# A hop later, and other queues: moving the substitution, the up weights and the gated stores of a hybrid RWKV-7 trunk

## The chip, the cores and the metric

The kernel runs on one core of a Trainium2 chip. The metric is device time in microseconds, the median of several executions. The core's engines run side by side, each with its own queue in order: TensorE (PE, with its weight loads PEld), VectorE (DVE), ScalarE (ACT), GpSimd (POOL) and SyncE (SP). A DMA is issued by one of the queues, here by SP or by ACT; an issue that waits holds up what is queued behind it on that engine.

## The reference, cut to what matters

One layer, 512 tokens, model width 2048, everything in float32:

```python
h = rms_norm(x, norm_g)
z = h @ w_in                         # r, k, v, two loras of 64 | gate | pool input | pool gate
zs = zs + (token_shift(zs) - zs) * mu
w_loglog = -softplus(-(w0 + tanh(wd) @ w_up)) - 0.5
decay = exp(-exp(w_loglog))
a = sigmoid(a0 + ad @ a_up)          # w_up, a_up: the "up weights", 64 x 1024 each
y = wkv7_scan(r, decay, k, v, kk, a) # 16 heads of 64; a delta-rule state, one step a token
y_rwkv = (head_group_norm(y) + bonus) * silu(g_rwkv)
y_pool = (causal_multiscale_pool(u) @ w_pool) * pool_scale * silu(g_pool)
x = x + concat(y_rwkv, y_pool) @ w_out
x = x + sigmoid(x @ w_pg + b_pg) * (p @ w_ple)
return rms_norm(x, final_g)
```

## The kernel before

**Products.** Each large product is made of three float32r matmuls (`mm3`): weights and data are split into a high part and a rest. For a weight chunk (`wsplit`, L127) SP loads `raw`, ACT casts it to `whi` (L132), DVE subtracts to get `wlo` (L133); each has four buffers. The input projection goes by 128 columns at a time (`zcols`), as a generator from which `pump(n)` takes n matmuls to fill the time of PE between the small steps of the recurrence.

**Rounds.** The 16 heads are worked in 8 pairs j. The 512 tokens of a pair are cut into 8 chunks of 64. `recur(j)` (L767) walks the chunks: per chunk a product `py` with the state, whose result DVE makes into `zs` (L799); a product `pu`, copied by ACT to `uv` (L813); a product `ps`, from which DVE makes the next state `sbd` (L825). After each of these three comes a hop: `step()` (L775), then a `pump`. The first chunk has no `py`, so there are 23 hops in a round: the 6th is that after `py` of the third chunk, the 21st that after `py` of the last.

**The substitution.** For the next pair, `scores(j+1)` (L620), run in the second hop, makes the masked products `mt`, writes their diagonal blocks to DRAM (`nd`, L651), and reads them back, copied to all partitions, as two tiles `n` (L656). `invert(j+1)` (L667) inverts 32 triangular blocks of 32x32 by 31 steps of two DVE instructions (L674, L678). `step()` takes them from that generator: from the hop after `HS` on, `HN` at each hop. What a hop takes is put on DVE behind `lead[0]`, the last `zs` or `sbd` (`tc.issue_after` puts what it encloses behind that instruction, on the same engine's queue). When the 31 steps are through, the next call writes the result to DRAM (`xd`, L682) and reads it back as `x1` (L689). `gather(j+1)` (L695) transposes a part of it to `y1` (L732) for the products `pq`, `pmv` and `px`.

**The up weights.** `load_ab(j)` (L348) loads 128 columns of `w_up` and `a_up`, each twice, for the two halves of the partitions, into `ur` and `ar`: four DMAs of 32 KB, issued by ACT. It is called for pair j+1 at the start of `prepare(j)` (L577), which runs ahead of the round of pair j-1. `decay_and_rate(j)` (L519), called from `gather(j-1)`, casts them on ACT (L524, L525) and subtracts on DVE (L526). All these tiles have one buffer.

**Stores.** The gated output of a pair (`gate_out` in `finish`, L893) and of a pool unit (`pool_unit`, L438) go to the DRAM tensor `yd`, 256 KB each, by ACT's queue. `load_y` (L947) reads them, by ACT's queue, for the output projection.

**Order.** PE's order in the rounds is that of the program (`pin`). On the other engines a scheduler orders the instructions when the program is built; it takes what is ready by its own estimate of times, and the program's order and `tc.high_priority` decide between ready ones. On the chip each queue then keeps that order, whatever comes late.

## Time and profile before

| | |
|---|---|
| median of 3 runs | 1085.23 us |
| the runs | 1085.23, 1083.53, 1088.02 us |
| the profiled execution | 1082.7 us |
| its span, first to last instruction | 1081.0 us |
| granted TensorE clock over the span | 0.998 |
| SP's DMA queue | 112.28 MB, 35.9% of 16 engines' span |
| ACT's DMA queue | 33.56 MB, 9.4% |
| the eight rounds | about 75 to 690 us |
| output projection and per-layer embedding | about 715 to 1081 us |

The times of instructions below come from the profiled execution. A row of a timeline has start and length in us, the engine, the line of the kernel, the operation, output and inputs by the program's names, shapes and count; in square brackets stands how long the engine was idle before it, and for what it waited. SPq and ACTq are DMA issues of these queues. A helper's line stands for all its callers: L157 is every matmul of `mm`.

### The profile page before, as it was taken

How to read it: one execution, taken by the hardware profiler on the slowest of the kernel's cores; microseconds unless marked ns; L12 is line 12 of the kernel's file. 1: busy time of each engine (PE TensorE's matmuls, PEld its weight loads, DVE VectorE, ACT ScalarE, POOL GpSimd, SP SyncE). 2: the span in 40 equal slices, each digit the busy share in tenths (PEclk: the TensorE clock that was granted, in tenths of full speed). 3: DMA queues.
4: the chain of work that ended last, by engine and by line, in shares of the span. 5: the costliest groups of instructions: out<-in, count | busy, mean ns of one | idle time of the engine just before them, and what ended most of it. 6: DMA issues, size and time to landing. Idle time of an engine off the chain costs nothing.

```text
span 1081.0 us, 17106 instructions
## 1 busy us (share of the span) xinstructions
PE 1056.6 (98%) x5996; PEld 872.1 (81%) x5996; DVE 714.0 (66%) x1851; ACT 441.5 (41%) x901; POOL 75.0 (7%) x180
## 2 busy tenths in 40 slices
PE   5999999999999999999999999999999999999996
PEld 4888878888888887878788788888888888888885
DVE  6676978888779789787887857563432424445356
ACT  7633435335335354353352344553222222333337
POOL 2100010110110100200101201000000000000000
PEclk9999999999999999999999999999999999999999
DMA  7434443342634533434435343774434428355434
GB/s 236 117 115 111 139 116 88 116 120 74 168 88 114 144 89 105 120 89 112 106 91 158 100 129 111 239 243 141 171 121 143 166 98 271 122 182 161 169 98 156
DMA packets 212916, 146.94 MB, mean 136 GB/s; under 512 B 68085, under 2 KB 173150, under 8 KB 212830
## 3 DMA queue, kind: packets, MB, share of 16 engines
q1 hardware_dynamic: 192126, 112.28, 35.9%
q10 hardware_dynamic: 20704, 33.56, 9.4%
q8 instruction: 47, 0.77, 0.3%
q14 instruction: 39, 0.32, 0.1%
HBM read 122.21 MB, written 23.07 MB: 134 GB/s over the span
## 4 chain that ended last, share of the span: by engine, by line
PE 91%; DVE 4%; DMA 3%; ACT 2%; issue 1%; ACTq 0%; SPq 0%; DVEq 0%
PE acc_o L157 16%; PE acc_g L157 16%; PE zb L157 14%; PE zv L157 8%; PE zg L157 8%; PE zr L157 8%; PE zk L157 7%; PE py L157 2%; PE pu L157 2%; PE pple L157 2%; PE pm L157 1%; DMA n<-nd 1%; PE pp L157 1%; PE ps L157 1%; DMA xt<-in_x_dram 1%; PE pmv L157 1%
## 5 line engine op out<-in xcount | busy, mean ns | idle before, releaser
L133 DVE TENSOR_TENSOR wlo_g<-raw_g,whi_g 128x512 fp32r<-128x512 f32 x84 | 57.0, 685 | 74.4 <-ACT whi_g L132 72.3
L157 PE MATMUL zb<-hhi,whi_b 128*128 128x512 f32 x256 | 106.0, 414 | 0.0
L133 DVE TENSOR_TENSOR wlo_o<-raw_o,whi_o 128x512 fp32r<-128x512 f32 x64 | 43.9, 690 | 90.9 <-ACT whi_o L132 90.8
L157 PE MATMUL zb<-hhi,wlo_b 128*128 128x512 f32 x256 | 100.4, 392 | 0.0
L157 PE MATMUL acc_o<-whi_o,ylo 128*128 128x512 f32 x256 | 100.2, 391 | 0.0
L157 PE MATMUL acc_o<-whi_o,yhi 128*128 128x512 f32 x256 | 99.9, 390 | 0.0
L157 PE MATMUL zb<-hlo,whi_b 128*128 128x512 f32 x256 | 99.8, 390 | 0.0
L157 PE MATMUL acc_o<-wlo_o,yhi 128*128 128x512 f32 x256 | 99.7, 389 | 0.0
L132 ACT CAST whi_g<-raw_g 128x512 fp32r<-128x512 f32 x84 | 52.0, 621 | 105.3 <-PE acc_g L157 58.9
L157 PE MATMUL acc_g<-whi_g,x2hi 128*128 128x512 f32 x208 | 81.2, 391 | 0.0
L832 POOL TENSOR_SCALAR s0p<-sbd,pw 64x64 f32<-64x64 f32 x96 | 58.0, 604 | 332.0 <-DVE sbd L825 243.5
L157 PE MATMUL acc_g<-wlo_g,x2hi 128*128 128x512 f32 x208 | 80.9, 389 | 0.0
L157 PE MATMUL acc_g<-whi_g,x2lo 128*128 128x512 f32 x208 | 80.6, 389 | 0.0
L132 ACT CAST whi_o<-raw_o 128x512 fp32r<-128x512 f32 x64 | 39.9, 623 | 96.3 <-PE acc_o L157 96.3
L132 ACT CAST whi_b<-raw_b 128x512 fp32r<-128x512 f32 x64 | 39.7, 621 | 86.7 <-PE zb L157 29.2
L133 DVE TENSOR_TENSOR wlo_b<-raw_b,whi_b 128x512 fp32r<-128x512 f32 x64 | 43.6, 683 | 27.3 <-ACT whi_b L132 27.1
L157 PEld LDWEIGHTS zb<-hhi,wlo_b 128*128 128x128 f32 x256 | 48.0, 188 | 10.9
L678 DVE TENSOR_TENSOR xw<-xw,tm 128x60 f32<-128x60 f32 (+24 forms) x248 | 52.1, 210 | 7.0
L157 PEld LDWEIGHTS acc_o<-wlo_o,yhi 128*128 128x128 f32 x256 | 48.1, 188 | 9.9
L157 PEld LDWEIGHTS acc_o<-whi_o,ylo 128*128 128x128 f32 x256 | 48.1, 188 | 9.8
L157 PEld LDWEIGHTS acc_o<-whi_o,yhi 128*128 128x128 f32 x256 | 48.1, 188 | 9.7
L157 PEld LDWEIGHTS zb<-hhi,whi_b 128*128 128x128 f32 x256 | 48.2, 188 | 8.3
(283 smaller groups left out, 2529.6 us busy)
## 6 DMA issues: line engine op xcount, KB each, us to landing
raw_b<-in_w_in_dram SPq DMA_DIRECT2D x64, 256.0 KB
raw_o<-in_w_out_dram SPq DMA_DIRECT2D x64, 256.0 KB
raw_g<-in_w_pg_dram SPq DMA_DIRECT2D x64, 256.0 KB
raw_k<-in_w_in_dram SPq DMA_DIRECT2D x32, 256.0 KB
raw_r<-in_w_in_dram SPq DMA_DIRECT2D x32, 256.0 KB
raw_v<-in_w_in_dram SPq DMA_DIRECT2D x32, 256.0 KB
raw_g<-in_w_in_dram SPq DMA_DIRECT2D x32, 256.0 KB
bkd<-bk SPq DMA_DIRECT2D x8, 512.0 KB
```

The source lines that it names most:

```text
L132: nc.scalar.copy(hi, raw)
L133: nc.vector.tensor_tensor(lo, raw, hi.bitcast(F32), ALU.subtract)
L157: i = nc.tensor.matmul(*a, **k)
L678: nc.vector.tensor_tensor(xw[:, 0:n_, s + 1:32], xw[:, 0:n_, s + 1:32], tm[:, 0:n_, 0:w_], ALU.add)
L832: nc.gpsimd.tensor_scalar(s0p[hc, :], nxt[hc, hc], pcn[hc], None, ALU.mult)
```

## The change

The substitution begins one hop later (`HS` 5 to 6), and at the 21st hop, the 15th of those in which it runs, three steps are taken in place of two. The up weights of the next pair are loaded after `scores` has issued the loads of `n`, behind the second of them on SP, and by SP in place of ACT. The stores of the gated outputs and of the pool branch are issued by SP in place of ACT.

```diff
@@ load_ab
-                nc.scalar.dma_start(out=raw[64 * h:64 * h + 64, :], in_=src[0, :, jc])
+                nc.sync.dma_start(out=raw[64 * h:64 * h + 64, :], in_=src[0, :, jc])
@@ pool_unit
-        nc.scalar.dma_start(out=yd[NJ + m], in_=sgp)
+        nc.sync.dma_start(out=yd[NJ + m], in_=sgp)
@@ prepare
-        if j + 1 < NJ:
-            load_ab(j + 1)
@@ scores
             nb.append(t_)
+        if j + 1 < NJ:
+            with tc.issue_after(n_.ins):
+                load_ab(j + 1)
         bg = rw.tile([P, NCH, 4, 32], F32, name=f"bg{j}", tag="bk")
@@ step
-                    for _ in range(HN):
+                    for _ in range(HN + (hop[0] == HE1)):
                         next(work, None)
@@ gate_out
-                nc.scalar.dma_start(out=yd[j], in_=yo)
+                nc.sync.dma_start(out=yd[j], in_=yo)
@@
-    HS, HN = 5, 2
+    HS, HN, HE1 = 6, 2, 21
```

## The prediction

> **What bounds the kernel now.** I read the page's engine shares first, then the waits of the tensor engine alone, then stretches of the span cut at the rounds over the eight head pairs.

> ```profile
> PE 1056.6 (98%) x5996; PEld 872.1 (81%) x5996; DVE 714.0 (66%) x1851; ACT 441.5 (41%) x901; POOL 75.0 (7%) x180
> ```

> PE has work in 98% of the span, and the order of its matmuls in the rounds is pinned by hand. The span can shorten only where PE stands still, or where its next matmul starts late.

> ```profile
> PE py L157 <- DVE sbd L825: 1.4, 2, 0.9
> PE px L157 <- issue: 1.1, 1, 1.1
> PE pu L157 <- DVE zs L799: 1.0, 2, 0.6
> ```

> ```profile
> 424.00:497.00 73.00, 70.95 (x459) 57.69 (x455) 59.59 (x181) 30.11 (x66) 8.76 (x15) 1.00 0.41 107
> 497.00:573.40 76.40, 75.53 (x489) 62.10 (x489) 62.31 (x181) 31.60 (x67) 7.43 (x15) 1.00 0.45 120
> 573.40:664.00 90.60, 89.88 (x561) 73.60 (x562) 64.45 (x203) 32.39 (x73) 11.80 (x18) 1.00 0.41 113
> ```

> The first view lists engine, waited-for, total us, times, longest: inside the rounds the large waits of PE are for sbd and zs, both made by the vector engine (DVE), and one of 1.1 us that the profile puts down to nothing. The second gives length, then the busy time of PE, its weight loads, DVE, ACT and POOL, the granted clock, the DMA share and GB/s. The three rounds idle 2.05, 0.87 and 0.72 us, 3.64 us together, at a granted clock of 1.00. So everything that this change can take away is a few microseconds of 1082.7; 5.4 us would be 0.5%, about the smallest difference that a measurement of this kernel can tell from none.

> What makes sbd late is seen in the order of DVE in one round:

> ```profile
> 509.02 0.29 DVE L799 TENSOR_TENSOR zs<-py,mv 64x128 f32<-64x128 f32 x1 [1.55 <-PE py L157]
> 509.35 0.69 DVE L133 TENSOR_TENSOR wlo_r<-raw_r,whi_r 128x512 fp32r<-128x512 f32 x1
> 512.26 0.19 DVE L674 TENSOR_TENSOR tm<-i,n 128x31 f32<-128x31 f32 x1 [2.21 <-DMA n<-nd]
> ...
> 513.81 0.19 DVE L674 TENSOR_TENSOR tm<-xw,n 128x29 f32<-128x29 f32 x1
> ...
> 514.48 0.19 DVE L678 TENSOR_TENSOR xw<-xw,tm 128x28 f32<-128x28 f32 x1
> 514.59 0.69 DVE L133 TENSOR_TENSOR wlo_v<-raw_v,whi_v 128x512 fp32r<-128x512 f32 x1
> 515.20 0.59 DVE L825 SCALAR_TENSOR_TENSOR sbd<-ps,pw,s0p 64x64 f32<-64x64 f32 x2
> ```

> After zs of the third chunk (the sixth hop), the first step of the substitution stands at the head of DVE's queue and waits 2.21 us for the load of n. Then come four steps (two of the sixth hop, two of the seventh: both are queued behind the same zs) and only then sbd, for which PE waits:

> ```profile
> 434.37 0.39 PE L157 MATMUL zk<-hhi,wlo_k 128*128 128x512 f32 x1
> 434.60 0.38 PE L157 MATMUL py<-sbd,ar 128*128 128x128 f32 x2
> ...
> 440.58 0.39 PE L157 MATMUL zr<-hhi,wlo_r 128*128 128x512 f32 x1
> 441.02 0.49 PE L157 MATMUL py<-sbd,ar 128*128 128x128 f32 x2
> ...
> 514.59 0.39 PE L157 MATMUL zr<-hhi,wlo_r 128*128 128x512 f32 x1
> 515.85 0.49 PE L157 MATMUL py<-sbd,ar 128*128 128x128 f32 x2 [0.87 <-DVE sbd L825]
> ...
> 589.43 0.39 PE L157 MATMUL zb<-hhi,wlo_b 128*128 128x512 f32 x1
> 590.34 0.49 PE L157 MATMUL py<-sbd,ar 128*128 128x128 f32 x2 [0.52 <-DVE sbd L825]
> ```

> An undisturbed py starts 0.23 us after the matmul before it (434.37 to 434.60). The other three start 0.44, 1.26 and 0.91 us after it: late by 0.21, 1.03 and 0.68 us, 1.92 us in all.

> **The change, part by part.** *The substitution a hop later.* With the start at hop 7, two steps stay behind zs, and the next two go behind sbd of hop 8. The two steps that leave the gap are the stretch from 513.81 to 514.67 (514.48 + 0.19) in the round shown: 0.86 us. The wait for n stays: hop 7 is queued behind the same zs. So sbd comes 0.86 us earlier, and the three late py are worth 0.21 + 0.86 + 0.68 = 1.75 us. Below: nothing, if DVE's queue fills the gap with other work; above: 1.92.

> *Three steps at hop 21.* Of the 31 steps, 30 ran by hop 20 before and one followed at hop 21; now 28 run by then and three follow. That is two steps, 0.86 us at the same price, more before the inverse can leave. It comes back through DRAM to the transposes y1, which PE needs for pq:

> ```profile
> 408.30 0.43 DVE L732 STREAM_TRANSPOSE y<-x 32x256 f32<-32x256 f32 x1
> ```

> ```profile
> 410.64 0.69 PE L157 MATMUL pq<-y,mt 32*32 32x32 f32 x32
> ```

> y1 is ready at 408.73, 1.91 us ahead of pq. A delay of 0.86 us is covered by this; in a round with no cover it costs 0.86 us, 6.0 us over seven. I take 0, since the cover shown is twice the delay.

> *Stores and up weights leave ACT's queue.* They issue there like this:

> ```profile
> 425.97 1.78 ACTq L354 DMA_DIRECT2D ar<-in_a_up_dram  x2
> ```

> ```profile
> 498.09 0.33 ACTq L893 DMA_DIRECT2D yd<-yo  x1
> ```

> A round's four weight DMAs and one store are at most 3.9 us of ACT's queue (4 x 0.89 + 0.33). In the waits of PE above no line names ACT, so by itself this gains 0; at most the 1.1 us of px, if that is ACT's. On SP it adds as much, and a store that waits for yo holds up the loads behind it. Those loads have room:

> ```profile
> 498.69 0.37 SPq L129 DMA_DIRECT2D raw_v<-in_w_in_dram  x1
> ...
> 505.74 1.19 SPq L656 DMA_DIRECT2D n<-nd  x2
> ```

> ```profile
> 510.63 0.42 ACT L813 COPY uv<-pu 64x64 f32<-64x64 f32 x2 [0.68 <-PE pu L157]
> 511.79 0.62 ACT L132 CAST whi_v<-raw_v 128x512 fp32r<-128x512 f32 x1 [0.74 <-PE zr L157]
> ```

> raw_v issues at 498.69 and its cast runs at 511.79, 13.1 us later, and that cast waits for PE, not for its load. The loads of bg, which now stand behind the weights, are read only by the transposes in the last chunk. So SP's extra issue is hidden, 0; without that cover it is up to 3.9 us in each of seven rounds, 27 us. The nd stores and the load of n stay ahead of the weights. The store of yo may come ahead of them, but nd waits for mt, which DVE makes after yo. The stores feed loads in the output projection only.

> *The up weights' casts and subtractions move too.* Their tiles have one buffer. Before, the loads refill them as soon as they are read, so the casts (L524, L525) and subtractions (L526) ran in the crowded stretch before the scores:

> ```profile
> 425.67 0.27 DVE L526 TENSOR_TENSOR as<-ar,as 64x128 fp32r<-64x128 f32 x1
> ```

> Now the loads wait for n's issue and the casts fall into the hops. Two subtractions, 0.54 us, leave the stretch in which DVE made PE wait for zs (1.0 us over two places above). I take 0.5 us from one of them; bounds 0 and 1.0. In the hops they can land ahead of sbd, and take back up to 0.54 us in each late round.

> **Sum:** 1.75 + 0.5 = 2.2 us off 1082.7 (span 1081.0, 1.7 around it): 1080.5. The median of the runs is 1085.2, 2.5 above the profiled execution, with runs from 1083.5 to 1088.0; from the median the forecast is **1083.0 us**.

> [...] The rows first:

> ```profile
> 434.00:435.00 1.00, 1.00 (x7) 0.87 (x6) 0.00 (x0) 0.00 (x0) 0.45 (x1) 1.00 0.26 67
> ```

> While n is in flight and little else, a quarter of the sixteen DMA engines is busy, at 67 GB/s. The two loads of n are 512 KB; at that rate they take 7.8 us, so from an issue at 505.74 the second is in at about 513.5. [...]

> **The rivals.**
> 1. *ACT stands still for the up weights* (the slower side). The weights issue behind n; a cast of them that was placed in ACT's queue for an earlier landing blocks what follows. Place: a cast of L524 ahead of the copy uv (L813), which releases ps:

> ```profile
> 512.52 0.38 PE L157 MATMUL ps<-uv,bkn 128*128 128x128 f32 x2
> ```

> The copy shown ends at 511.05, 1.47 us ahead of ps. Held until 513.5 it ends at 513.92, 2.87 us later, so PE waits 1.40 us in that round. The point: two rounds of seven eat the gain of 2.2. With all seven the time is 1085.2 + 9.8 - 2.2 = 1092.8, and each further microsecond of landing adds 7. For it: DVE's wait of 2.21 us for n shows that a queue here can be ordered for an earlier landing than the chip gives. Against: ACT is busy 41% of the span, and a cast that falls behind the copy waits at no cost until the next one.
> 2. *Nothing moves*: DVE fills the gap before sbd with the moved subtractions and further weight splits, or the last steps make y1 late by what the first ones gain. 1085.2.
> 3. *The shifted queues also dissolve what I leave standing*: all of the 3.64 us of idle time above, the 1.1 of px included. A stop costs more than its idle mark: the two marked py are late by 1.03 and 0.68 with marks of 0.87 and 0.52, 0.16 more each. For the five waits in the view of PE that is 0.8, and the unmarked py adds 0.21: together 4.65, or 1080.6. For it: DVE's crowded stretch is relieved at both ends. Against: the change touches nothing that px waits for except ACT's queue.
> 4. *The change does not do what it says*: with hop 7 behind the same zs the wait for n of 2.2 us remains; then only the two steps count. This is inside the forecast.

> **Chances.** Forecast 0.48, nothing 0.20 (rival 2), more 0.16 (rival 3), slower 0.16 (rival 1); rival 4 has its chance inside the forecast. The range leaves out the larger part of rival 1 and the end of rival 3, and allows for the scatter of the runs: **1078.5 to 1088.5**; the likeliest case alone is 1081.5 to 1084.5. Faster by over 0.5% (below 1079.8): the better part of rival 3 with the scatter of the runs, and a little of the forecast's low end, 0.13. Slower by over 0.5% (above 1090.7): rival 1 in six rounds or more, or in fewer with a later landing, 0.12. Within 0.5%: 0.75.

> **What would show it.** Right: in the seven rounds one pair of steps fewer between zs of the third chunk and sbd, py 0.23 us after its predecessor, the wait for n still there, the idle time of PE in the three stretches near 1.8 (3.64 less the two marks of 1.39 and the 0.5) instead of 3.64, and SP's weight and store issues without a later cast. Wrong: PE waiting for uv's ps or for pu, with ACT or DVE idle for a load of up weights; pq waiting for y1; a raw weight's cast that waits for its load.

## The result, and the profile after

| | before | after |
|---|---|---|
| median of 6 runs each, side by side | 1085.61 us | 1116.88 us |
| the runs | 1083.21 to 1088.02 | 1114.17 to 1118.08 |
| ratio, 95% interval | | 1.0287 [1.0266, 1.0308] |
| span of the profiled execution | 1081.0 us | 1115.8 us |

The change costs 31 us. The forecast was 1083.0 with a range to 1088.5: wrong, in sign and in size. The first line of the page of the changed kernel, and the waits of PE (engine, what it waited for, total us, times, longest):

```profile
PE 1066.7 (96%) x5996; PEld 878.4 (79%) x5996; DVE 714.4 (64%) x1851; ACT 440.3 (39%) x901; POOL 74.4 (7%) x180
```

```profile
PE ps L157 <- ACT uv L814: 25.2, 6, 4.9
...
PE py L157 <- DVE sbd L826: 0.8, 2, 0.6
PE px L157 <- issue: 0.8, 1, 0.8
...
PE pu L157 <- DVE zs L800: 0.7, 2, 0.5
```

The number of instructions is the same on every engine. The waits that the prediction worked with (py, px, pu) have all shrunk. One wait is new, and it alone is 25.2 us: PE waits for `ps`, that is for ACT's copy `uv`, in six rounds. ACT is no busier than before (440.3 us against 441.5), so the copy was late for another reason. The same view of all engines names it:

```profile
ACT uaz L525 <- DMA ur<-in_w_up_dram: 50.4, 7, 9.0
```

Six of these seven waits fall into the rounds; the seventh ends at 92.21, before the first copy `uv`, and costs PE nothing.

One of the six rounds, first on the queues of SP and ACT, then on PE (start, length, engine, line, operation; in brackets the idle time before it and what ended it):

```profile
533.76 1.18 SPq L654 DMA_DIRECT2D n<-nd  x2
534.99 0.52 SPq L354 DMA_DIRECT2D ur<-in_w_up_dram  x1
535.55 0.58 SPq L129 DMA_DIRECT2D raw_v<-in_w_in_dram  x1
536.17 0.52 SPq L354 DMA_DIRECT2D ur<-in_w_up_dram  x1
536.73 1.24 SPq L354 DMA_DIRECT2D ar<-in_a_up_dram  x2
```

```profile
537.52 0.69 ACT L369 ACTIVATE sk<-zk,dprm 128x512 f32<-128x512 f32 x1
543.99 0.30 ACT L525 CAST uaz<-ur 64x128 fp32r<-64x128 f32 x1 [5.77 <-DMA ur<-in_w_up_dram]
544.92 0.30 ACT L524 CAST us<-ur 128x128 fp32r<-128x128 f32 x1 [0.64 <-DMA ur<-in_w_up_dram]
545.25 0.42 ACT L814 COPY uv<-pu 64x64 f32<-64x64 f32 x2
```

```profile
540.55 0.40 PE L157 MATMUL zr<-hhi,wlo_r 128*128 128x512 f32 x1
545.72 0.80 PE L157 MATMUL ps<-uv,bkn 128*128 128x128 f32 x2 [4.78 <-ACT uv L814]
...
549.30 0.63 PE L157 MATMUL zr<-hlo,whi_r 128*128 128x512 f32 x1
549.73 0.60 PE L157 MATMUL zr<-hhi,wlo_r 128*128 128x512 f32 x1
550.16 0.39 PE L157 MATMUL py<-sbd,ar 128*128 128x128 f32 x2
```

The casts of `ur` stand in ACT's queue ahead of `uv`. The second half of `ur` is issued by 536.69 and the cast that needs it can start only at 544.92, 8.2 us later. Until then `uv`, which waits for nothing but its place in the queue, is held, and PE with it. `ps` was due at 540.78 (540.55 and the 0.23 us between matmuls) and starts at 545.72: 4.94 us late.

The stop costs more than its length. After it, matmuls start 0.43 us apart (549.30, 549.73, 550.16) in place of 0.23. From the start of `ps` to that of the next `py` there are 4.44 us and nine matmuls of zr; the same ten steps before the change, from the `ps` at 512.52 to 0.23 us behind the zr at 514.59, took 2.30. So 2.14 us more are lost to the clock. The stretches of the span show it (length; PE, weight loads, DVE, ACT, POOL; granted clock, DMA share, GB/s):

```profile
547.00:550.20 3.20, 3.20 (x9) 2.43 (x9) 1.93 (x7) 0.23 (x2) 0.91 (x2) 0.51 0.34 92
550.20:552.00 1.80, 1.80 (x12) 1.55 (x11) 1.34 (x5) 0.39 (x1) 0.00 (x0) 1.00 0.35 55
```

Granted clock 0.51, then 1.00. The six stops have idle marks of 4.63, 4.72, 4.91, 3.33, 2.86 and 4.78 us; all but the one of 2.86 are followed by such slow matmuls. **The account:** marks 25.2, and 0.16 us each beside the mark, make 26.2. The first thirty matmuls behind each stop take 2.31, 1.67, 1.66, 1.51, 0.76 and 2.14 us longer than the same ones in the run with the casts behind the fourth chunk's copy (below), in which PE runs the same matmuls in the same order without these stops. The 0.76, behind the stop of 2.86, is not the clock but a `py` that waits for `sbd`. These six are 10.1 us, with the stops 36.3 of the 37.0 us between the spans of the two executions (1115.8 and 1078.9). Beside the kernel before, the difference is 34.8 us between the profiled spans and 31 between the medians.

The length of a stop doesn't decide by itself whether slow matmuls follow it: behind one of 2.04 us in another run they did, behind one of 3.08 they didn't (at the end of this text).

The seventh round, which has no cast of up weights (the last load is issued in the sixth), runs as before:

```profile
601.00:692.00 91.00, 90.56 (x565) 74.12 (x564) 67.94 (x208) 33.04 (x74) 12.61 (x18) 1.00 0.44 123
```

PE idles 0.44 us of 91.00 in it, at clock 1.00.

### The profile page after: what moved, and what is told of

It is laid out like the page before. It is cut to its first block, busy times and chain, and to the rows that moved or that the text cites. A ratio compares the mean times of both kernels' runs of the same rounds, so it can differ in the third digit from the quotient of the medians.

```text
span 1115.8 us, 17123 instructions
## 1 busy us (share of the span) xinstructions
PE 1066.7 (96%) x5996; PEld 878.4 (79%) x5996; DVE 714.4 (64%) x1851; ACT 440.3 (39%) x901; POOL 74.4 (7%) x180
## 4 chain that ended last, share of the span: by engine, by line
PE 82%; DMA 8%; DVE 5%; ACT 2%; issue 1%; SPq 1%; ACTq 0%; DVEq 0%
PE acc_g L157 15%; PE acc_o L157 15%; PE zb L157 12%; PE zv L157 8%; PE zr L157 8%; PE zk L157 6%; PE zg L157 6%; DMA ur<-in_w_up_dram 4%; PE py L157 2%; DMA yin<-yd 2%; PE pple L157 2%; PE pu L157 1%; PE ps L157 1%; PE pm L157 1%; PE pp L157 1%
## 5 line engine op out<-in xcount | busy, mean ns | idle before, releaser
L157 PE MATMUL zb<-hhi,whi_b 128*128 128x512 f32 x256 | 106.0, 414 | 0.0
L133 DVE TENSOR_TENSOR wlo_g<-raw_g,whi_g 128x512 fp32r<-128x512 f32 x84 | 57.0, 684 | 72.5 <-ACT whi_g L132 70.0
L133 DVE TENSOR_TENSOR wlo_o<-raw_o,whi_o 128x512 fp32r<-128x512 f32 x64 | 43.7, 690 | 90.3 <-ACT whi_o L132 90.3
L157 PE MATMUL zb<-hhi,wlo_b 128*128 128x512 f32 x256 | 100.4, 392 | 0.0
L157 PE MATMUL acc_o<-whi_o,ylo 128*128 128x512 f32 x256 | 100.2, 391 | 0.0
L157 PE MATMUL acc_o<-whi_o,yhi 128*128 128x512 f32 x256 | 100.0, 391 | 0.2 <-ACT whi_o L132 0.2
L157 PE MATMUL acc_o<-wlo_o,yhi 128*128 128x512 f32 x256 | 99.8, 390 | 0.3 <-DVE wlo_o L133 0.3
L157 PE MATMUL zb<-hlo,whi_b 128*128 128x512 f32 x256 | 99.8, 390 | 0.0
L132 ACT CAST whi_g<-raw_g 128x512 fp32r<-128x512 f32 x84 | 52.0, 621 | 104.8 <-PE acc_g L157 55.8
L157 PE MATMUL acc_g<-whi_g,x2hi 128*128 128x512 f32 x208 | 81.2, 391 | 0.0
L157 PE MATMUL acc_g<-wlo_g,x2hi 128*128 128x512 f32 x208 | 80.9, 389 | 0.0
L157 PE MATMUL acc_g<-whi_g,x2lo 128*128 128x512 f32 x208 | 80.7, 389 | 0.0
L132 ACT CAST whi_o<-raw_o 128x512 fp32r<-128x512 f32 x64 | 39.6, 623 | 95.7 <-PE acc_o L157 95.7
L132 ACT CAST whi_b<-raw_b 128x512 fp32r<-128x512 f32 x64 | 39.7, 620 | 83.7 <-PE zb L157 30.7
L133 DVE TENSOR_TENSOR wlo_b<-raw_b,whi_b 128x512 fp32r<-128x512 f32 x64 | 43.8, 686 | 23.7 <-ACT whi_b L132 23.4
L157 PEld LDWEIGHTS zb<-hhi,wlo_b 128*128 128x128 f32 x256 | 48.0, 188 | 10.9
L157 PEld LDWEIGHTS acc_o<-wlo_o,yhi 128*128 128x128 f32 x256 | 48.1, 188 | 10.6 <-DVE wlo_o L133 0.6
L157 PEld LDWEIGHTS acc_o<-whi_o,yhi 128*128 128x128 f32 x256 | 48.1, 188 | 10.3 <-ACT whi_o L132 0.6
L157 PE MATMUL zk<-hhi,whi_k 128*128 128x512 f32 x128 | 55.7, 435 | 0.0
L157 PEld LDWEIGHTS acc_o<-whi_o,ylo 128*128 128x128 f32 x256 | 48.1, 188 | 9.7
```

The costliest lines, as they stand in the source:

```text
L132: nc.scalar.copy(hi, raw)
L133: nc.vector.tensor_tensor(lo, raw, hi.bitcast(F32), ALU.subtract)
L157: i = nc.tensor.matmul(*a, **k)
```

## The experiments

Theory: the loss is rival 1 of the prediction, ACT's queue held by casts whose load lands behind `n`. What had to be told apart: which part of the change does it; whether the queue, the place of the issue, or the place of the casts; and what delays the landing. Each run is beside runs of the kernel before on the same chip.

### The substitution alone

```diff
-                    for _ in range(HN):
+                    for _ in range(HN + (hop[0] == HE1)):
...
-    HS, HN = 5, 2
+    HS, HN, HE1 = 6, 2, 21
```

> Only the substitution's start (seventh hop, three steps at the 21st); stores and up weights as before. Theory A, that the up weights landing behind n hold up ACT: no wait of PE for uv, 1083 us by the forecast's own sum (1.8 us less than before), certainly within 1080 to 1087. Theory B, that the later and denser steps are the cost: most of the 31 us, 1105 to 1116.

Measured: 1082.46 us, ratio 0.9984 [0.9975, 0.9994]: of 1085 us that is 1.7 [0.7, 2.7]. The waits of PE:

```profile
PE pq L157 <- DVE y L732: 0.5, 1, 0.5
...
PE py L157 <- DVE sbd L825: 0.2, 1, 0.2
```

The wait for sbd fell from 1.4 to 0.2 us. One pq waits 0.5 us for y1, which is what three steps at hop 21 can cost.

### The stores alone

```diff
@@ pool_unit
-        nc.scalar.dma_start(out=yd[NJ + m], in_=sgp)
+        nc.sync.dma_start(out=yd[NJ + m], in_=sgp)
@@ gate_out
-                nc.scalar.dma_start(out=yd[j], in_=yo)
+                nc.sync.dma_start(out=yd[j], in_=yo)
```

> Only the gated stores by SP. Theory A: 0, 1083 to 1088. Theory C, that what SP takes over holds up its loads (a store that waits in front of weight loads or of nd and n): a part of the 31 us, over 1090, with casts that wait for raw loads.

Measured: 1086.09 us, ratio 1.0013 [0.9999, 1.0027]. No effect that can be told from none.

### The up weights alone

The kernel before with this part of the change:

```diff
-                nc.scalar.dma_start(out=raw[64 * h:64 * h + 64, :], in_=src[0, :, jc])
+                nc.sync.dma_start(out=raw[64 * h:64 * h + 64, :], in_=src[0, :, jc])
@@ prepare
-        if j + 1 < NJ:
-            load_ab(j + 1)
@@ scores
+        if j + 1 < NJ:
+            with tc.issue_after(n_.ins):
+                load_ab(j + 1)
```

> Only the up weights, by SP and behind n; substitution and stores as before. Theory A: all of it, 1112 to 1122, ACT waiting for ur some 50 us and PE for uv some 25 us. Theories B and C alone: 1084 to 1090.

Measured: 1116.36 us, ratio 1.0292 [1.0274, 1.0310]. PE's waits: `ps` for `uv`, 24.5 us in six places. The whole loss sits in this part.

### The whole change, but the up weights early

The edit against the changed kernel; the issue stays with SP:

```diff
@@ prepare
+        if j + 1 < NJ:
+            load_ab(j + 1)
@@ scores
-        if j + 1 < NJ:
-            with tc.issue_after(n_.ins):
-                load_ab(j + 1)
```

> The whole change, except that the up weights are loaded at the start of prepare as before, but by SP. Theory A: the loss is in the place, not in the queue: 1081 to 1086, no wait for ur. Theory C: SP is the wrong queue at any place: over 1095.

Measured: 1082.77 us, ratio 0.9973 [0.9958, 0.9987], and no wait for `ur`. So SP's queue is innocent: what costs comes with the late place of the loads in the round.

### The whole change, with the casts late

```diff
@@ prepare_key
-        split(kqh, kql, kk)
+        keyed[0] = split(kqh, kql, kk)
@@ decay_and_rate
-            nc.scalar.copy(st, raw)
-            nc.scalar.copy(z_[hi, :], raw[hi, :])
+            with tc.issue_after(keyed[0].ins):
+                nc.scalar.copy(st, raw)
+                nc.scalar.copy(z_[hi, :], raw[hi, :])
```

> The whole change, with the casts of the up weights put on ACT behind the cast kqh of the gather (what their place was before), so that they stand behind all copies uv of the round; the loads land as late as in the change. Theory A (the block in ACT's queue is the price, not the landing): 1081 to 1088, no wait of PE for uv. Rival A2 (the late landing or the extra traffic behind n itself costs, whatever ACT does): above 1100.

Measured: 1090.93 us, ratio 1.0069 [1.0049, 1.0090]. No wait for `uv` is left, and most of the loss is gone with it, but the time misses what was expected. PE's waits, and one place on PE:

```profile
PE pu L157 <- DVE us L527: 5.1, 6, 1.4
PE pa L157 <- DVE ve L144: 2.4, 3, 0.8
```

```profile
554.11 0.40 PE L157 MATMUL zb<-hhi,wlo_b 128*128 128x512 f32 x1
555.25 0.50 PE L157 MATMUL pu<-uhh,us 128*128 128x512 f32 x1 [0.75 <-DVE us L527]
```

The casts now come just before the product that reads them, and the subtraction between is late: two new waits, 7.5 us in all. The profile puts the second, that of `pa`, down to `ve`, which DVE runs right behind the late subtraction of `as`, an operand of `pa`. The run didn't show whether the place behind `n` costs anything by itself; the run with the casts behind the fourth chunk's copy does.

### The weights behind n, issued by ACT

The changed kernel, with the loads ordered behind the issue of `n`, but without a wait:

```diff
-                nc.sync.dma_start(out=raw[64 * h:64 * h + 64, :], in_=src[0, :, jc])
+                d_ = nc.scalar.dma_start(out=raw[64 * h:64 * h + 64, :], in_=src[0, :, jc])
+                if of is not None:
+                    tc.add_manual_dep(d_.ins, of.ins.name, mybir.DependencyInfo(mybir.DependencyClass.NoSync,
+                                                                                mybir.DependencyReason.DATA))
@@ scores
-            with tc.issue_after(n_.ins):
-                load_ab(j + 1)
+            load_ab(j + 1, n_)
```

The question is what makes the up weights land late in the changed kernel. If it is SP's queue, in which they stand behind `n`, 1084 to 1096 us were expected here.

> [...] If four busy DMA engines or the late place alone are the reason, they land as late as in the change: 1108 to 1120.

Measured: 1107.81 us, ratio 1.0211 [1.0183, 1.0239], between the two expectations. The wait for `uv` is 16.5 us in six places. On ACT:

```profile
529.89 1.45 ACTq L354 DMA_DIRECT2D ar<-in_a_up_dram  x2
...
537.58 0.30 ACT L527 CAST as<-ar 128x128 fp32r<-128x128 f32 x1 [0.74 <-DMA ar<-in_a_up_dram]
...
538.10 0.42 ACT L816 COPY uv<-pu 64x64 f32<-64x64 f32 x2
```

The issue ends at 531.34 and the waiting cast starts at 537.58, 6.2 us later against 8.2. In the changed kernel, where SP issues both, `n` is first used at 540.70 and `ur`, issued behind it, at 543.99. But ACT's queue gives back only a third of the wait for `uv` (16.5 us against 25.2); the records of single DMA packets narrow down what else holds the weights there. Those of `n` run from 529.64 to 537.10, those of the weights from 529.99 to 537.01, so the weights aren't behind `n`, but the last of them come in only with the last of `n`; it is alike in the other five rounds. Why so few packets are stretched over that time, the run doesn't show.

### Each load of n in four parts

The changed kernel, with each load of `n` as four DMAs of 32 partitions. That they keep more of the DMA engines busy than the quarter (0.26) seen in the flight of `n` before was the author's estimate.

```diff
-            n_ = nc.sync.dma_start(out=t_, in_=nd[:, :, :, 16 * i:16 * i + 16, :].rearrange(
-                "a b u r c -> (a b u) r c").unsqueeze(0).to_broadcast([4, 32, 16, 32]))
+            for q in range(4):
+                n_ = nc.sync.dma_start(out=t_[32 * q:32 * q + 32], in_=nd[:, :, :, 16 * i:16 * i + 16, :].rearrange(
+                    "a b u r c -> (a b u) r c"))
```

> [...] If n's four busy engines hold the up weights back, n lands sooner, DMA share in its flight is over 0.5, the wait for ur falls from 50 us to under 25 and the time to 1085 to 1100. If the weights are late for another reason (SP's issues, bg's traffic, DRAM): 1110 to 1120. The six more issues on SP cost up to 3.6 us ahead of the weights.

Measured, with the rest of the change: 1081.05 us, ratio 0.9973 [0.9963, 0.9982], faster than the 1085 to 1100 expected. No wait for `uv`. On SP and ACT:

```profile
510.71 0.52 SPq L354 DMA_DIRECT2D ur<-in_w_up_dram  x1
512.37 0.38 SPq L129 DMA_DIRECT2D raw_b<-in_w_in_dram  x1
512.79 0.52 SPq L354 DMA_DIRECT2D ur<-in_w_up_dram  x1
```

```profile
509.83 0.42 ACT L815 COPY uv<-pu 64x64 f32<-64x64 f32 x2 [0.68 <-PE pu L157]
...
514.51 0.29 ACT L525 CAST uaz<-ur 64x128 fp32r<-64x128 f32 x1
515.61 0.30 ACT L524 CAST us<-ur 128x128 fp32r<-128x128 f32 x1 [0.80 <-DMA ur<-in_w_up_dram]
516.04 0.42 ACT L815 COPY uv<-pu 64x64 f32<-64x64 f32 x2
```

Two things changed here at once. `ur` lands 2.3 us after its issue (513.31 to 515.61) in place of 8.2. And the casts moved: they now stand behind the copy `uv` of the third chunk, ahead of that of the fourth, since the order is made from the scheduler's estimates and more issues stand before the weights. At their old place they would still have held a copy that ran at 509.83, before `ur` was even issued. So this run doesn't tell landing from place. Nor does it show by itself how many DMA engines `n` keeps busy: from 505 to 511 us, with loads of `raw_v` among those of `n`, the DMA share is 0.54.

### n in four parts, the weights early

The run before, with the up weights at the start of `prepare`:

```diff
@@ prepare
+        if j + 1 < NJ:
+            load_ab(j + 1)
@@ scores
-        if j + 1 < NJ:
-            with tc.issue_after(n_.ins):
-                load_ab(j + 1)
```

> The loads of n in four parts as in the run before this one, up weights early by SP, stores by SP, substitution from the seventh hop. Theory A: no wait for ur; the wait of DVE for n (18.4 us in the kernel before) falls below 10 us; 1080 to 1085, perhaps the fastest of all.

Measured: 1081.66 us, ratio 0.9980 [0.9970, 0.9989]. DVE's wait for `n` fell to 2.5 us in all (23.6 in the changed kernel), and that changes nothing on PE's path that the time shows.

### The casts behind the fourth chunk's copy

This settles what the run with the late casts left open. `u_` is the copy `uv`: `n` in two loads, the weights behind it on SP, all as in the change; only the casts stand about 6 us later in ACT's queue.

```diff
@@ recur
-                    nc.scalar.copy(uv[pb:pb + 64, ch, hc], psu[hc, hc])
+                    u_ = nc.scalar.copy(uv[pb:pb + 64, ch, hc], psu[hc, hc])
+            if ch == 3:
+                fourth[0] = u_
@@ decay_and_rate
-            nc.scalar.copy(st, raw)
-            nc.scalar.copy(z_[hi, :], raw[hi, :])
+            with tc.issue_after(fourth[0].ins) if fourth[0] is not None else tc.high_priority(offset=0):
+                nc.scalar.copy(st, raw)
+                nc.scalar.copy(z_[hi, :], raw[hi, :])
```

> The changed kernel in full, with weights behind n on SP and n in two DMAs, but the four casts of the up weights stand in ACT's queue right behind the copy uv of the fourth chunk, one chunk later than in the changed kernel. By the theory that the loss is a cast of a load that lands 10 us after n's issue, standing in ACT's queue ahead of the copy uv of the third chunk: the fourth chunk's copy runs about 6 us later, when the weights are in, so no copy is held up, PE waits for no uv, and the time is 1081 to 1086. By the rival that the weights' place behind n costs by itself (PE or DVE late for another reason, or shared DMA engines): 1100 or more. By the rival that the later casts are late for pu, as where they stood behind the cast of kqh: 1088 to 1094.

Measured: 1081.31 us, ratio 0.9974 [0.9963, 0.9985], as the theory said. On ACT:

```profile
509.70 0.42 ACT L817 COPY uv<-pu 64x64 f32<-64x64 f32 x2 [0.68 <-PE pu L157]
...
515.91 0.43 ACT L817 COPY uv<-pu 64x64 f32<-64x64 f32 x2 [1.44 <-PE pu L157]
516.38 0.30 ACT L527 CAST us<-ur 128x128 fp32r<-128x128 f32 x1
```

Both copies wait only for PE, and the cast for nothing. The late landing costs nothing as such; the whole loss is the place of four short casts in an in-order queue, with the subtractions on DVE that wait for them.

### The weights ahead of n

The changed kernel, with the up weights between the stores of `nd` and the loads of `n`; `load_ab` returns its last load, and `n` is issued behind it:

```diff
@@ scores
+        if j + 1 < NJ:
+            with tc.issue_after(nd_.ins):
+                nd_ = load_ab(j + 1)
         nb = []
...
-        if j + 1 < NJ:
-            with tc.issue_after(n_.ins):
-                load_ab(j + 1)
```

> The changed kernel, with the up weights issued by SP at the same point of the program but between the stores of nd and the loads of n. By the theory that n's narrow transfer is what holds the weights: they land some 3 us after their issue, before the copy uv of the third chunk, PE waits for uv at most a few tenths per round, and the time is 1081 to 1088. By the rival that any issue at that point of the round is too late for the place that the casts get: PE still waits for uv 2 us or more per round, 1100 or more.

Measured: 1086.89 us, ratio 1.0023 [1.0009, 1.0037], in the range of the theory. SP, ACT and DVE in one round:

```profile
510.19 1.15 SPq L354 DMA_DIRECT2D ar<-in_a_up_dram  x2
```

```profile
510.46 0.30 ACT L526 CAST uaz<-ur 64x128 fp32r<-64x128 f32 x1 [1.48 <-DMA ur<-in_w_up_dram]
510.66 0.62 ACT L132 CAST whi_r<-raw_r 128x512 fp32r<-128x512 f32 x1
...
513.24 0.30 ACT L525 CAST as<-ar 128x128 fp32r<-128x128 f32 x1 [1.76 <-DMA ar<-in_a_up_dram]
```

```profile
511.31 0.69 DVE L133 TENSOR_TENSOR wlo_r<-raw_r,whi_r 128x512 fp32r<-128x512 f32 x1 [3.42 <-ACT whi_r L132]
511.92 0.59 DVE L828 SCALAR_TENSOR_TENSOR sbd<-ps,pw,s0p 64x64 f32<-64x64 f32 x2
```

Not behind `n`, `ar` lands 1.9 us after its issue (511.34 to 513.24). The casts still stand too early and hold up a cast of a raw weight, which holds DVE's subtraction, behind which stands sbd; PE's wait for sbd is 5.4 us in six places here. The same fault at a smaller price.

### The substitution and n in four parts, nothing else

The kernel before, with the edits of the first run and of the first with `n` in four parts.

> The kernel before with the substitution a hop later and each load of n cut into four DMAs of 32 partitions; the up weights early and by ACT, the stores by ACT. The candidate for the best: the two gains that were measured, the hop (1082.5) and the wide n (1081.1 with the rest of the change). If they add, 1080 to 1081.5; if the wide n only repairs what the late weights broke, 1082 to 1083, as the hop alone.

Measured: 1081.01 us, ratio 0.9972 [0.9963, 0.9982], in the range for gains that add, but its interval isn't clear of that of the hop alone. By 0.3% it beats the kernel before, but so do the hop alone, the whole change with the weights early, both other runs with `n` in four parts, and the casts behind the fourth copy; all these intervals overlap, so none can be called the best.

## Why the prediction was wrong, step by step

- **The substitution a hop later: right.** Forecast 1.75 us, measured by itself 1.7 [0.7, 2.7]. In the changed kernel two steps stand between zs and sbd, and DVE still waits for `n`, as forecast:

```profile
537.28 0.29 DVE L800 TENSOR_TENSOR zs<-py,mv 64x128 f32<-64x128 f32 x1 [1.55 <-PE py L157]
...
540.70 0.19 DVE L675 TENSOR_TENSOR tm<-i,n 128x31 f32<-128x31 f32 x1 [1.62 <-DMA n<-nd]
...
545.80 0.19 DVE L675 TENSOR_TENSOR tm<-xw,n 128x30 f32<-128x30 f32 x1
...
547.64 0.59 DVE L826 SCALAR_TENSOR_TENSOR sbd<-ps,pw,s0p 64x64 f32<-64x64 f32 x2
```

- **Three steps at hop 21: nearly right.** Taken at 0; one pq of the run with the hop alone waits 0.5 us, none in the changed kernel.
- **Stores on SP: right.** 0 was forecast, and none could be measured. px still waited 1.1 us in that run, and in the one with the weights early and by SP, so its wait wasn't these issues of ACT's.
- **The up weights: wrong, and this is the step that failed.** "Now the loads wait for n's issue and the casts fall into the hops", valued at a gain of 0.5 us. The price in the hops was sought on DVE only (subtractions ahead of sbd, "up to 0.54 us in each late round"), and the casts on ACT went into rival 1. They stood ahead of `uv` in all six rounds that have them. The seventh round that the rival counted has none: `scores` of the last pair loads no more weights.
- **Rival 1: the right mechanism, mis-sized.** Place, waiting engine and releaser are as it said. Its price was 1.40 us a round; the round shown cost 4.94 + 2.14 = 7.08. First, the landing: it let the cast go when `n` is in, 7.8 us after the issue, which is the bytes over the rate alone. That the weights come in no sooner than `n`, on which its 1.40 us rests, was the author's assumption and no run of before shows it; in the changed kernel `n` is first used at 540.70 and `ur` at 543.99. By the packets' records the first packet of `n` starts 1.4 us after the issue; the last ends 9.40 us after it in the round of the kernel before that the rival took (515.14), and 9.45 in this one (543.21). The weights come behind it, with a load of `raw_v` between their halves: `us` could start at 544.92, 11.2 us after `n`'s issue, 3.4 later than counted, about half of it `n`'s own. That is nearly the whole of the 3.5 us between the wait of 1.40 and the one of 4.94. Second, the clock: nothing in the prediction priced a stop beyond its mark but 0.16 us, and the longest wait quoted from the rounds of the kernel before was 1.1 us.
- **Its chance: too low.** The argument against it, that "ACT is busy 41% of the span", says nothing about an in-order queue: ACT stood idle for 5.77 us in the round shown, with the copy behind the waiting cast.
- **The rest of the sum, 1.75 us, was sound.** The whole change with the weights early, which leaves that step out, has a ratio of 0.9973 [0.9958, 0.9987]: of 1085 us that is 2.9 [1.4, 4.6]. With the weights late and the casts behind the fourth copy it is 2.6 us faster than its runs of before (1083.88 to 1081.31). No run shows a gain of 0.5 us by moved subtractions: between these two runs no difference can be told.

What stays open: how much of the repair by `n` in four parts is the faster landing and how much the new place of the casts, and why weights issued by ACT still come in only with the last of `n` (537.01 us against 537.10 in the round shown).

## What to carry to other kernels

When a load is moved later, follow its first reader, not only its queue: the reader's place in an in-order engine's queue is settled when the program is built, and if the load lands after that place comes up, everything behind the reader waits, however idle the engine is (here ACT idled 5.77 us, with the copy `uv` behind the cast). Tie such a reader behind the last urgent instruction that can run before the landing, with room before its own deadline; here 6 us later cost nothing, ahead of `uv` cost 31 us, and just before `pu` cost 7.5 us of waits. And price a stop of PE of two microseconds or more at its length plus the slow matmuls that can follow it, here 1.5 to 2.3 us behind five stops of six.

## What the runs showed of the hardware

```profile
302.30:304.30 2.00, 0.00 (x0) 0.00 (x0) 1.76 (x7) 1.03 (x5) 0.00 (x0) 1.00 0.29 85
304.30:307.00 2.70, 2.69 (x8) 2.21 (x9) 1.87 (x7) 0.89 (x2) 1.42 (x2) 0.57 0.70 159
535.50:538.50 3.00, 0.00 (x0) 0.00 (x0) 2.33 (x8) 1.62 (x6) 0.00 (x0) 1.00 0.61 157
538.50:541.00 2.50, 2.43 (x12) 2.05 (x13) 1.69 (x7) 0.69 (x3) 0.75 (x2) 1.00 0.40 71
```

  The granted clock behind the first is 0.57, behind the second 1.00. The clock's records show what goes with it. In the changed kernel half clock begins at 150.81, 232.73, 311.24, 389.74, 543.34 and 1109.95 us. Those beginnings are 24, 23, 23, 45 and 166 steps of 3.41 us apart, and it lasts 6.83, 3.41, 3.41, 3.41, 6.83 and, at the end of the span, 7.92 us. In the run with the weights issued by ACT the stop of 2.04 us lies whole in one step (301.26 to 304.67); that of 3.08 is cut by the edge at 536.77, and PE idles 1.28 and 1.80 us in the two steps. Over the thirteen traces, from 40 us on, half clock followed each of the 28 such steps at full clock in which PE idled 1.90 us or more (13 of them at the ends of the spans), and of the others only two (1.11 us in the run with the weights early, 1.54 in that with the casts late), which stay unexplained. In the changed kernel alone, the six steps that half clock followed have 2.40 to 3.41 us of idling, and the most without it is 1.89.
- A load of 32 KB, from the end of its issue to the cast that waited for it: 1.8 to 2.3 us ahead of `n` (second half of `ar`, five rounds of the run with the weights ahead of it), 5.7 to 6.6 us beside the loads of `n` from the other queue (the same half, six rounds of the run with the weights issued by ACT), and 7.8 to 9.1 us directly behind them in the same queue (first half of `ur`, six rounds of the changed kernel).
